# Moving the GpSimd work between the output projections and the up-projections to VectorE and ScalarE

## The chip, the cores and the metric

The kernel runs on one core of one Trainium2 chip. The metric is the device time of one execution in microseconds, as the median of several runs. Five engines run programs of their own: TensorE (PE, with its weight loads as PEld), VectorE (DVE), ScalarE (ACT), GpSimd (POOL) and SyncE (SP), which issues nearly all transfers. Each works through its own list of instructions in order, and semaphores tie the lists together.

## The reference

A trunk of two layers on 1024 positions with 1024 channels. Each layer has a mixer (even: sparse attention beside a gated convolution; odd: causal pooling beside latent attention) with one output projection, and then a convolutional FFN. Both sub-layers end in a scaled residual and a LayerNorm:

```python
h = x * (1.0 + sc_f) + sh_f
y = conv_ffn(h, ffn_w_up[l], ffn_conv_w[l], ffn_w_down[l])
x = layer_norm(DN_ALPHA * x + (1.0 + g_f) * y, ln_ffn_g[l], ln_ffn_b[l])

def conv_ffn(h, w_up, conv_w, w_down):
    u = causal_dwconv(h @ w_up, conv_w)
    val, gate = u[..., :D_FF], u[..., D_FF:]
    return (jax.nn.silu(gate) * val) @ w_down
```

D_FF is 2816, so the up-projection has 22 pairs (value and gate) of 128 columns.

## The kernel before

Positions are cut into two halves of 512 columns (`HALF`), channels into eight blocks (`KD`) of 128 partitions. A product in full precision is made of three matmuls on a high and a low half of each operand (`mm3`, L289 to L291). So every operand is first split: ACT copies the high half (`split`, L267), and DVE or POOL subtracts it from the source for the low half (L268).

The stretch that the change touches comes once in each layer:

- **Output projection** (`out_proj`). For each half, eight weight tiles `w_evo` or `w_odo` of 128x1024; the second half's low halves are POOL's. After each tile, `Norm.residual` loads the residual `xa` (in layer 0 scaled on POOL, L484), DVE adds the gated product (L495), and POOL sums the eight tiles for the mean (L505).
- **Norm**. `Norm.mean` subtracts the mean (DVE, L529), squares on ACT (L535), sums the squares on DVE and POOL in turn (L536). `Norm.var` multiplies by rstd (DVE, L556), writes the residual `xo` (ACT, L563), makes the next input `h32` (POOL, L572), and splits it to `h_f`.
- **Plain up-projections** (`Ffn.plain`). The first four pairs (`PLAIN`), half by half. The second half takes its weights' low halves from POOL. Beside it, `sums` forms the operands `t` of the Strassen products from the two halves (L772, L773, L778 and four splits on POOL). `activate` is the convolution: for each tile one ACT instruction (L701), two on DVE (L703), a silu (ACT, L707) and a product (DVE, L708).
- **Strassen up-projections** (`Ffn.strassen`). The other 18 pairs, one unit each, with seven products of 12 matmuls (84 a unit) in place of eight. `prepare` makes the operands of a unit one unit ahead: POOL forms s1 (L834, from `rawg`), s2 (L835, from s1 and `raw_upv`), s3 (L841) and s4 (L842); ACT and DVE split them. `fetch` loads `raw_upv` into one of two buffers, so that unit n's load can start when unit n-2's last reader, the split of s4 (`wl<-raw_upv`), has gone. `out` copies the products from PSUM to `u` on ACT (L873) or adds them on DVE (L871). In layer 0, `between` also works three steps of the next layer's modulation a unit, two reductions on DVE (L378) and two loads `mod_raw` to a step.

Then the down-projection (`dn`) follows, which uses `prepare` too (under the name "dn") and ends in a norm.

PE's list is written by hand. The lists of the other engines are put in order by a scheduler, by the priorities in the code (`tc.high_priority`).

Of the kernel before, what the change touches and what calls it, by code (L numbers as in the profile page):

```python
# [14 lines left out]
AF = mybir.ActivationFunctionType  # L15
# [192 lines left out]
def trunk(ctx, tc, t, out):  # L208
# [250 lines left out]
    class Norm:  # L459
# [20 lines left out]
        def residual(self, dt, ps):  # L480
            xa = self.st.tmp.tile([P, HALF], F32, tag="xa", name="xa")
            if self.first:
                load(xa, t["xT"][dt, :, half(self.hf)])
                G.tensor_scalar(xa, xa, ALPHA, 0.0, ALU.mult, ALU.add)  # L484
            else:
                load(xa, xa_dram[self.hf, dt])
            self.r[dt] = self.st.r.tile([P, HALF], F32, tag="r", name="r")
            self.gated(dt, ps, xa)
# [10 lines left out]
        def add(self, n, order=range(KD)):  # L499

            r = self.r[order[n]]
            if n:
                eng = V if self.end and n >= KD - 1 else G
                with tc.high_priority(offset=AHEAD):
                    eng.tensor_tensor(self.acc, self.r[order[0]] if n == 1 else self.acc, r, ALU.add)  # L505

# [5 lines left out]
        def mean(self):  # L512
# [14 lines left out]
            with tc.high_priority(offset=2 * AHEAD):  # L527
                for dt in range(KD):
# [4 lines left out]
                    else:  # L533
                        sq = self.tile("sq", "sq")
                        A.activation(sq, r[dt], AF.Square)  # L535
                        (G if e else V).tensor_tensor(acc[e], acc[e], sq, ALU.add)  # L536
            self.sq = acc
            defer(self.delays[1], self.var)

        def var(self):  # L540
# [14 lines left out]
            for dt in PAIRED:  # L555
# [11 lines left out]
                if self.h is None:  # L567
# [3 lines left out]
                h32 = r[dt] if self.keep else self.tile("h32", "h32")  # L571
                G.tensor_scalar(  # L572
                    h32, r[dt], f[:, 2, dt : dt + 1], f[:, 3, dt : dt + 1], ALU.mult, ALU.add
                )
# [63 lines left out]
    def out_proj(st, wsrc, k0, ysplit, gate, f, first):  # L638
        for hf in range(2):
# [4 lines left out]
            for dt in range(KD):  # L644
                src = t[wsrc][dt][:, ks[0] * P : (ks[-1] + 1) * P]
                w = weights(src, f"{wsrc}_{hf}_{dt}", lo_eng="pool" if hf else "dve")
                ps = bank("oproj")
# [22 lines left out]
    class Ffn:  # L670
# [40 lines left out]
        def plain(self):  # L711
# [3 lines left out]
            with ExitStack() as s:  # L715
# [4 lines left out]
                for hf in range(2):  # L720
# [3 lines left out]
                    for pr in range(PLAIN):  # L724
                        last = hf and pr == PLAIN - 1
                        w, ps = [], []
                        for n in range(2):
                            c = pr + n * NPAIR
                            w.append(weights(t["w_up"][l, c], f"up{l}_{hf}_{c}", "pool" if hf else "dve"))
                            ps.append(bank("up"))  # L730
# [31 lines left out]
        def sums(self):  # L762
# [5 lines left out]
            for k in range(4):  # L768
                b11, b21 = (st.tmp.tile([P, HALF], F32, tag="h32", name="blk") for _ in range(2))
                b12, b22 = st.kept[k], st.kept[k + 4]  # L770
                b = st.t[0].bitcast(F32)
                G.tensor_tensor(b11, b[:, 0, k], b[:, 1, k], ALU.add)  # L772
                G.tensor_tensor(b21, b[:, 0, k + 4], b[:, 1, k + 4], ALU.add)  # L773
                t1 = st.tmp.tile([P, HALF], F32, tag=("xa", "acc")[k // 2], name="t1")
                V.tensor_tensor(t1, b12, b11, ALU.subtract)
                V.tensor_tensor(b12, b22, b12, ALU.subtract)
                V.tensor_tensor(b22, b22, t1, ALU.subtract)
                G.tensor_tensor(b21, b21, b22, ALU.subtract)  # L778
                for dst, src in ((self.t2, b22), (self.t3, b12), (self.t4, b21)):
                    x = dst[k]  # L780
                    split(x[:, 0], x[:, 1], src, "pool" if dst is self.t4 else "dve")
                self.t1.append(t1)
# [36 lines left out]
        def prepare(self, n, name):  # L819
# [10 lines left out]

            c0, c1 = slice(0, m), slice(m, 2 * m)
            with tc.high_priority(offset=AHEAD):
                s1, s2 = (tmp.tile([P, HALF], F32, tag="s", name="s", bufs=2)[:, :m] for _ in "12")
                G.tensor_tensor(s1, g[:, c0], g[:, c1], ALU.add)  # L834
                G.tensor_tensor(s2, s1, v[:, c0], ALU.subtract)  # L835
                a = divide(v, 2 * m, f"{name}a{self.l}_{n}")
# [3 lines left out]
                split(hi[:, c1], lo[:, c1], s1)  # L840
                G.tensor_tensor(g[:, c0], v[:, c0], g[:, c0], ALU.subtract)  # L841
                G.tensor_tensor(v[:, c1], v[:, c1], s2, ALU.subtract)  # L842
                self.w = {
# [1334 lines left out]
```

## Time and profile before

| what | value |
|---|---|
| median of 3 runs | 2623.29 us (2621.45 to 2625.12) |
| the profiled execution | 2616.24 us, its span 2614.4 us |
| PE busy | 2375.9 us (91%) |
| DVE busy | 2169.9 us (83%) |
| ACT busy | 1378.1 us (53%) |
| POOL busy | 1078.8 us (41%) |

The profiled execution is 7.05 us under the median of the runs. Shares are means over the whole span; the stretch in question has values of its own. A PE that is busy isn't a PE at its peak, since matmuls overlap.

### The profile page before, as it was taken

How to read it: one execution, taken by the hardware profiler on the slowest of the kernel's cores; microseconds unless marked ns; L12 is line 12 of the kernel's file. 1: busy time of each engine (PE TensorE's matmuls, PEld its weight loads, DVE VectorE, ACT ScalarE, POOL GpSimd, SP SyncE). 2: the span in 40 equal slices, each digit the busy share in tenths (PEclk: the TensorE clock that was granted, in tenths of full speed). 3: DMA queues.
4: the chain of work that ended last, by engine and by line, in shares of the span. 5: the costliest groups of instructions: out<-in, count | busy, mean ns of one | idle time of the engine just before them, and what ended most of it. 6: DMA issues, size and time to landing. Idle time of an engine off the chain costs nothing. (4 is left out here: it accounts for less than half of the span.)

```text
span 2614.4 us, 32451 instructions
## 1 busy us (share of the span) xinstructions
PE 2375.9 (91%) x10762; PEld 1905.7 (73%) x10762; DVE 2169.9 (83%) x3495; ACT 1378.1 (53%) x2449; POOL 1078.8 (41%) x816
## 2 busy tenths in 40 slices
PE   6799997989978988998999898998989999998997
PEld 4678785877656767876787677887666888876786
DVE  7868888886898999988977868786798877788976
ACT  4558734884644344553434547675555555563434
POOL 0000003757663222324537535554675333334536
PEclk9999998999989999999999999999989999999999
DMA  6513320225434555344314331224432322244313
GB/s 249 170 42 108 97 69 17 74 77 163 133 107 159 183 172 162 104 132 151 91 55 130 93 111 39 68 80 151 138 110 93 109 84 82 93 139 140 100 48 107
DMA packets 126473, 289.44 MB, mean 111 GB/s; under 512 B 16032, under 2 KB 23712, under 8 KB 125408
## 3 DMA queue, kind: packets, MB, share of 16 engines
q1 hardware_dynamic: 125152, 283.16, 34.3%
q10 hardware_dynamic: 1152, 4.19, 0.5%
q8 instruction: 85, 1.39, 0.2%
q14 instruction: 84, 0.69, 0.1%
HBM read 234.87 MB, written 48.23 MB: 108 GB/s over the span
## 5 line engine op out<-in xcount | busy, mean ns | idle before, releaser
L703 DVE SCALAR_TENSOR_TENSOR cv<-u,taps,cv 128x512 f32<-128x512 f32 x352 | 308.4, 902 | 18.1 <-ACT cv L701 16.4
L834 POOL TENSOR_TENSOR s<-rawg 128x512 f32<-128x512 f32 (+3 forms) x60 | 78.4, 1307 | 258.8 <-DVE wlo_ups L268 87.1
L268 POOL TENSOR_TENSOR v<-v,v 128x512 fp32r<-128x512 f32 x8 | 11.9, 1492 | 416.9 <-ACT v L267 416.9
L999 DVE SCALAR_TENSOR_TENSOR r<-dn,mod,r 128x512 f32<-128x512 f32 x198 | 147.0, 745 | 41.8 <-PE dn L291 39.8
L701 ACT ACTIVATE cv<-u,taps 128x512 f32<-128x512 f32 x176 | 124.3, 721 | 56.4 <-DMA z<-cv 29.0
L289 PE MATMUL up<-t,wh 128*128 128x512 f32 x288 | 119.3, 414 | 31.5 <-ACT u L873 31.5
L707 ACT ACTIVATE cv<-cv 128x512 f32<-128x512 f32 x88 | 55.6, 632 | 144.4 <-DVE cv L703 143.5
L290 PE MATMUL up<-h_f,whi_up 128*128 128x512 f32 x256 | 105.6, 412 | 25.7 <-DVE h_f L268 25.7
L873 ACT COPY u<-up 128x512 f32<-128x512 f32 x144 | 83.9, 584 | 77.3 <-issue 33.3
L378 DVE CUSTOM_DVE_ANT_0 mod_raw<-mod_raw,cond_row 128x512 f32<-128x512 f32 (+1 forms) x112 | 106.0, 953 | 20.1 <-DMA mod_raw<-in_ada_w 16.1
L268 DVE TENSOR_TENSOR wl<-rawg,wh 128x512 fp32r<-128x512 f32 (+3 forms) x120 | 119.7, 1000 | 2.6 <-ACT wh L267 2.6
L290 PE MATMUL up<-t,wh 128*128 128x512 f32 x288 | 117.9, 409 | 0.0
L291 PE MATMUL up<-t,wl 128*128 128x512 f32 x288 | 117.6, 408 | 0.0
L835 POOL TENSOR_TENSOR s<-s,raw_upv 128x512 f32<-128x512 f32 x36 | 50.5, 1403 | 161.0 <-DMA raw_upv<-in_w_up 138.7
L267 ACT CAST wh<-rawg 128x512 fp32r<-128x512 f32 (+3 forms) x120 | 65.0, 545 | 98.2 <-PE dn L290 51.3
L289 PE MATMUL up<-h_f,whi_upa 128*128 128x512 f32 x288 | 114.5, 398 | 0.8 <-ACT whi_upa L267 0.8
L291 PE MATMUL up<-h_f,wlo_upa 128*128 128x512 f32 x288 | 113.7, 395 | 0.7 <-DVE wlo_upa L268 0.7
L290 PE MATMUL up<-h_f,whi_upa 128*128 128x512 f32 x288 | 113.0, 392 | 0.0
L268 DVE TENSOR_TENSOR pl<-pt,ph 128x128 fp32r<-128x128 f32 (+2 forms) x192 | 99.6, 545 | 14.8 <-ACT ph L267 14.1
L291 PE MATMUL up<-h_f,wlo_up 128*128 128x512 f32 x256 | 104.1, 407 | 6.0 <-POOL wlo_up L268 6.0
L842 POOL TENSOR_TENSOR raw_upv<-raw_upv,s 128x512 f32<-128x512 f32 x36 | 60.3, 1675 | 118.7 <-DVE wlo_upa L268 118.7
L289 PE MATMUL up<-h_f,whi_up 128*128 128x512 f32 x256 | 106.0, 414 | 1.6 <-ACT whi_up L267 0.8
(755 smaller groups left out, 8562.7 us busy)
## 6 DMA issues: line engine op xcount, KB each, us to landing
mod_raw<-in_ada_w SPq DMA_DIRECT2D x96, 256.0 KB, 2.9
z<-cv SPq DMA_DIRECT2D x88, 256.0 KB, 2.0
raw_upv<-in_w_up SPq DMA_DIRECT2D x36, 512.0 KB, 3.7
rawg<-in_w_up SPq DMA_DIRECT2D x34, 512.0 KB, 3.7
raw_up<-in_w_up SPq DMA_DIRECT2D x32, 512.0 KB, 3.7
z<-z SPq DMA_DIRECT2D x56, 256.0 KB, 2.7
xa_dram<-xo SPq DMA_DIRECT2D x48, 256.0 KB, 2.3
raw_dr<-in_w_dr SPq DMA_DIRECT2D x32, 384.0 KB, 3.1
```

The costliest lines, as they stand in the source:

```text
L267: A.copy(hi, src)
L268: (V if lo_eng == "dve" else G).tensor_tensor(lo, src, hi.bitcast(F32), ALU.subtract)
L289: T.matmul(ps, lhsT=wh, rhs=xh, start=start, stop=False, skip_group_check=more)
L290: T.matmul(ps, lhsT=wh, rhs=xl, start=False, stop=False, skip_group_check=more)
L291: T.matmul(ps, lhsT=wl, rhs=xh, start=False, stop=stop, skip_group_check=more)
L378: V.tensor_tensor_reduce(out=raw, in0=raw, in1=self.cond[:, o], scale=1.0, scalar=0.0, op0=ALU.mult, op1=ALU.add, accum_out=self.acc[:, j, ...
L701: A.activation(y[n], u[:, 0:HALF], AF.Copy, scale=self.taps[:, c, 0:1])
L703: V.scalar_tensor_tensor(y[n], u[:, k : k + HALF], self.taps[:, c, k : k + 1], y[n], ALU.mult, ALU.add,)
L834: G.tensor_tensor(s1, g[:, c0], g[:, c1], ALU.add)
L842: G.tensor_tensor(v[:, c1], v[:, c1], s2, ALU.subtract)
L873: A.copy(dst, ps)
L999: V.scalar_tensor_tensor(r, ps, self.gate[:, dt : dt + 1], r, ALU.mult, ALU.add)
```

## The change

All of POOL's work in this stretch goes to DVE, but for two kinds that go to ACT: the scaling of the residual in layer 0, and the next input h32. In `prepare` the four sums move for "up" alone; for "dn" they stay. `Norm` is also used at the ends of the FFNs, so its sums and h32 move there as well.

```diff
             if self.first:
                 load(xa, t["xT"][dt, :, half(self.hf)])
-                G.tensor_scalar(xa, xa, ALPHA, 0.0, ALU.mult, ALU.add)
+                A.mul(xa, xa, ALPHA)
...
             if n:
-                eng = V if self.end and n >= KD - 1 else G
                 with tc.high_priority(offset=AHEAD):
-                    eng.tensor_tensor(self.acc, self.r[order[0]] if n == 1 else self.acc, r, ALU.add)
+                    V.tensor_tensor(self.acc, self.r[order[0]] if n == 1 else self.acc, r, ALU.add)
...
-                        (G if e else V).tensor_tensor(acc[e], acc[e], sq, ALU.add)
+                        V.tensor_tensor(acc[e], acc[e], sq, ALU.add)
...
-                G.tensor_scalar(
-                    h32, r[dt], f[:, 2, dt : dt + 1], f[:, 3, dt : dt + 1], ALU.mult, ALU.add
+                A.activation(
+                    h32, r[dt], AF.Identity, bias=f[:, 3, dt : dt + 1],
+                    scale=f[:, 2, dt : dt + 1],
                 )
...
-                w = weights(src, f"{wsrc}_{hf}_{dt}", lo_eng="pool" if hf else "dve")
+                w = weights(src, f"{wsrc}_{hf}_{dt}")
...
-                            w.append(weights(t["w_up"][l, c], f"up{l}_{hf}_{c}", "pool" if hf else "dve"))
+                            w.append(weights(t["w_up"][l, c], f"up{l}_{hf}_{c}"))
...
-                G.tensor_tensor(b11, b[:, 0, k], b[:, 1, k], ALU.add)
-                G.tensor_tensor(b21, b[:, 0, k + 4], b[:, 1, k + 4], ALU.add)
+                V.tensor_tensor(b11, b[:, 0, k], b[:, 1, k], ALU.add)
+                V.tensor_tensor(b21, b[:, 0, k + 4], b[:, 1, k + 4], ALU.add)
...
-                G.tensor_tensor(b21, b21, b22, ALU.subtract)
+                V.tensor_tensor(b21, b21, b22, ALU.subtract)
...
-                    split(x[:, 0], x[:, 1], src, "pool" if dst is self.t4 else "dve")
+                    split(x[:, 0], x[:, 1], src)
...
+            eng = V if name == "up" else G
...
-                G.tensor_tensor(s1, g[:, c0], g[:, c1], ALU.add)
-                G.tensor_tensor(s2, s1, v[:, c0], ALU.subtract)
+                eng.tensor_tensor(s1, g[:, c0], g[:, c1], ALU.add)
+                eng.tensor_tensor(s2, s1, v[:, c0], ALU.subtract)
...
-                G.tensor_tensor(g[:, c0], v[:, c0], g[:, c0], ALU.subtract)
-                G.tensor_tensor(v[:, c1], v[:, c1], s2, ALU.subtract)
+                eng.tensor_tensor(g[:, c0], v[:, c0], g[:, c0], ALU.subtract)
+                eng.tensor_tensor(v[:, c1], v[:, c1], s2, ALU.subtract)
```

PE's list stays as it was. Line numbers from L485 on shift by one or two. Three places show what the scheduler made of it.

The first is DVE's list in layer 1, where unit 7 of the Strassen products is prepared and the convolution of an earlier unit (`cv`) runs; `raw_upv` is the raw value weight, `wlo_ups` the low half of s1 and s2. Before:

```order
L268 TENSOR_TENSOR wlo_ups_7_17641<-s,whi_ups_7_17640 128x512 x2
L268 TENSOR_TENSOR wl<-raw_upv_6_17391,wh 128x512
L703 SCALAR_TENSOR_TENSOR cv<-u,taps_16437,cv 128x512 x4
L914 MEMSET u 128x2
L708 TENSOR_TENSOR cv<-cv 128x512
L871 TENSOR_TENSOR u<-up,u 128x512
L268 TENSOR_TENSOR wl<-rawg,wh 128x512
```

And of the change:

```order
L268 TENSOR_TENSOR wlo_ups_7_17641<-s,whi_ups_7_17640 128x512 x2
L835 TENSOR_TENSOR s<-rawg 128x512
L268 TENSOR_TENSOR wl<-raw_upv_6_17391,wh 128x512
L703 SCALAR_TENSOR_TENSOR cv<-u,taps_16437,cv 128x512 x4
L836 TENSOR_TENSOR s<-s,raw_upv_8_17660 128x512
L842 TENSOR_TENSOR rawg<-raw_upv_8_17660,rawg 128x512
L915 MEMSET u 128x2
L708 TENSOR_TENSOR cv<-cv 128x512
L872 TENSOR_TENSOR u<-up,u 128x512
L268 TENSOR_TENSOR wl<-rawg,wh 128x512
```

The sum s2 of unit 8 (now L836) stands four convolution steps behind the split that frees the buffer for its load, and in front of the next product and the next add from PSUM.

The second is the same place in layer 0, where the reductions of the modulation (L378, here as ISA) are mixed in. Before:

```order
L268 TENSOR_TENSOR wl<-raw_upv_6_6889,wh 128x512
L703 SCALAR_TENSOR_TENSOR cv<-u,taps_5935,cv 128x512 x2
L378 ISA mod_raw,mod_acc<-mod_raw,cond_row_6922 128x512
L378 ISA mod_acc 128x1
L703 SCALAR_TENSOR_TENSOR cv<-u,taps_5935,cv 128x512 x2
L378 ISA mod_raw,mod_acc<-mod_raw,cond_row_6922 128x512
L378 ISA mod_acc 128x1
L871 TENSOR_TENSOR u<-up,u 128x512
```

And of the change:

```order
L268 TENSOR_TENSOR wl<-raw_upv_6_6889,wh 128x512
L378 ISA mod_raw,mod_acc<-mod_raw,cond_row_6922 128x512
L378 ISA mod_acc 128x1
L835 TENSOR_TENSOR s<-rawg 128x512
...
L703 SCALAR_TENSOR_TENSOR cv<-u,taps_5935,cv 128x512 x3
L872 TENSOR_TENSOR u<-up,u 128x512
L268 TENSOR_TENSOR wl<-rawg,wh 128x512
L703 SCALAR_TENSOR_TENSOR cv<-u,taps_5935,cv 128x512
L836 TENSOR_TENSOR s<-s,raw_upv_8_7200 128x512
```

Here ten instructions stand between the two (the rows left out hold one more L378 and one sum of 8 columns). From one preparation to the next the list held 9 reductions in most units before, up to unit 15; now it holds 6 or 7, up to unit 19.

The third is ACT's list in layer 0 behind the second norm's square root; `xo` is the residual, `h_f` the split input. Before:

```order
L549 ACTIVATE rstd<-ln_var,eps_ln 128x512
L267 CAST whi_up_0_3_6296<-raw_up_0_3_6294 128x1024
L743 COPY u<-up 128x512
L563 ACTIVATE xo<-r,fm_5280 128x512 x2
L701 ACTIVATE cv<-u,taps_5935 128x512
L267 CAST h_f_1_5290<-r 128x512 x2
```

And of the change:

```order
L548 ACTIVATE rstd<-ln_var,eps_ln 128x512
L562 ACTIVATE xo<-r,fm_5280 128x512 x2
L571 ACTIVATE r<-r,fm_5280 128x512
L267 CAST whi_up_0_3_6296<-raw_up_0_3_6294 128x1024
L743 COPY u<-up 128x512
L571 ACTIVATE r<-r,fm_5280 128x512
L267 CAST h_f_1_5290<-r 128x512
```

The two h32 (L571) now stand in ACT's own list, ahead of the casts that read them.

## Rows read from the trace of the kernel before

**Rows 1.** Busy time by stretch: output projection, plain, Strassen; layer 0, then 1.

```profile
584.50:658.30 73.80, 69.97 (x297) 54.99 (x296) 50.49 (x55) 32.49 (x47) 55.26 (x36) 1.00 0.52 165
658.30:779.00 120.70, 98.61 (x391) 74.93 (x390) 111.76 (x131) 66.15 (x99) 75.95 (x41) 0.93 0.33 102
779.00:1181.70 402.70, 367.40 (x1514) 292.07 (x1513) 366.98 (x605) 191.73 (x314) 129.08 (x83) 0.96 0.48 153
1792.70:1867.50 74.80, 69.92 (x298) 54.86 (x297) 49.22 (x58) 34.20 (x49) 51.53 (x31) 1.00 0.63 204
1867.50:1985.70 118.20, 98.85 (x392) 75.72 (x391) 110.14 (x128) 66.31 (x99) 72.56 (x38) 0.93 0.33 104
1985.70:2349.30 363.60, 355.82 (x1514) 286.00 (x1513) 293.17 (x391) 196.75 (x313) 130.32 (x82) 0.99 0.30 98
```

The columns are the stretch, its length, then busy time (and instructions) of PE, PEld, DVE, ACT and POOL, PE's granted clock as a share of full speed, the transfers' share and their GB/s.

**Rows 2.** The same view inside the Strassen stretches: layer 0's first units, layer 1.

```profile
795.20:1027.40 232.20, 209.73 (x856) 166.16 (x856) 215.47 (x401) 97.58 (x160) 69.74 (x44) 0.95 0.54 173
2018.00:2288.00 270.00, 270.00 (x1167) 218.76 (x1166) 214.06 (x294) 141.52 (x222) 91.40 (x59) 1.00 0.28 92
```

**Rows 3.** Who waited for whom, layer 0's Strassen stretch: total us, times, longest.

```profile
PE up L289 <- ACT u L873: 27.9, 11, 5.5
...
ACT cv L707 <- DVE cv L703: 85.2, 18, 9.3
```

**Rows 4.** Timeline of single instructions, layer 0: start, duration, engine, line.

```profile
957.93 0.69 DVE L268 TENSOR_TENSOR wl<-raw_upv,wh 128x512 fp32r<-128x512 f32 x1
...
963.83 1.76 DVE L378 CUSTOM_DVE_ANT_0 mod_raw<-mod_raw,cond_row 128x512 f32<-128x512 f32 x1
...
967.22 0.74 DVE L703 SCALAR_TENSOR_TENSOR cv<-u,taps,cv 128x512 f32<-128x512 f32 x1
967.89 0.68 DVE L378 CUSTOM_DVE_ANT_0 mod_raw<-mod_raw,cond_row 128x512 f32<-128x512 f32 x1
...
968.50 1.22 DVE L268 TENSOR_TENSOR wlo_upa<-raw_upv,whi_upa 128x1024 fp32r<-128x1024 f32 x1
...
963.25 1.79 POOL L835 TENSOR_TENSOR s<-s,raw_upv 128x512 f32<-128x512 f32 x1 [6.45 <-DMA raw_upv<-in_w_up]
```

**Rows 5.** Groups of DVE instructions, layer 0's Strassen stretch: count, busy, mean ns.

```profile
L703 DVE SCALAR_TENSOR_TENSOR cv<-u,taps,cv 128x512 f32<-128x512 f32 x141 | 110.8, 811 | 3.1 <-ACT cv L701 2.7
L378 DVE CUSTOM_DVE_ANT_0 mod_raw<-mod_raw,cond_row 128x512 f32<-128x512 f32 x96 | 86.5, 909 | 18.2 <-DMA mod_raw<-in_ada_w 14.3 <-ACT cond_row L357 3.4
L268 DVE TENSOR_TENSOR wl<-rawg,wh 128x512 fp32r<-128x512 f32 x34 | 37.4, 1103 | 0.2 <-ACT wh L267 0.2
```

**Rows 6.** The same view of the plain stretch of layer 0.

```profile
L703 DVE SCALAR_TENSOR_TENSOR cv<-u,taps,cv 128x512 f32<-128x512 f32 x29 | 33.5, 1156 | 1.9 <-ACT cv L701 1.8
L268 DVE TENSOR_TENSOR t<-r,t 128x512 fp32r<-128x512 f32 x8 | 10.6, 1358 | 0.0
L708 DVE TENSOR_TENSOR cv<-cv 128x512 f32<-128x512 f32 x7 | 10.3, 1468 | 0.7 <-ACT cv L707 0.5
```

**Rows 7.** Groups of POOL and ACT instructions in the plain stretch of layer 0.

```profile
L572 POOL TENSOR_SCALAR r<-r,fm 128x512 f32<-128x512 f32 x8 | 15.8, 1984 | 11.5 <-ACT xo L563 11.5
...
L563 ACT ACTIVATE xo<-r,fm 128x512 f32<-128x512 f32 x8 | 6.3, 806 | 1.0 <-DVE r L556 1.0
```

**Rows 8.** PE's waits in the plain stretch of layer 0.

```profile
PE up L290 <- DVE h_f L268: 12.5, 3, 10.9
PE ln_mean L515 <- POOL ln_acc L505: 3.9, 1, 3.9
```

**Rows 9.** Timeline of layer 1, DVE and POOL, where a unit's load is awaited.

```profile
2092.43 0.69 DVE L268 TENSOR_TENSOR wl<-raw_upv,wh 128x512 fp32r<-128x512 f32 x1 [1.20 <-ACT wh L267]
2093.67 2.74 DVE L703 SCALAR_TENSOR_TENSOR cv<-u,taps,cv 128x512 f32<-128x512 f32 x4 [0.55 <-ACT cv L701]
...
2097.56 0.69 DVE L871 TENSOR_TENSOR u<-up,u 128x512 f32<-128x512 f32 x1 [0.42 <-PE up L291]
...
2096.99 1.31 POOL L835 TENSOR_TENSOR s<-s,raw_upv 128x512 f32<-128x512 f32 x1 [4.62 <-DMA raw_upv<-in_w_up]
```

## The prediction

> **What bounds the kernel now.** I read the busy time by stretch first. A matmul takes its place on PE every 270.00 / 1167 = 0.231 us where PE never pauses [rows 2]. So the 1514 matmuls of a Strassen stretch need 350 us, and the 391 of a plain one 90.5. Layer 1's Strassen stretch has 363.6, so PE bounds it; layer 0's has 402.7 and the plain ones 120.7 and 118.2, where DVE is busy for 91 to 93% [rows 1]. The reader should see that the same products take 39 us more where DVE also reduces the modulation.
>
> Then the waits, for how DVE's load reaches PE. In layer 0's Strassen stretch PE waits 27.9 us for ACT's copy `u` out of PSUM. ACT is only half busy there, but its list is in order: the silu L707 waits 85.2 us for DVE's convolution [rows 3], and the copy stands behind it. In the plain stretch PE waits 12.5 us for `h_f`, a low half made on DVE, and 3.9 for POOL's sum [rows 8].
>
> Then the timeline, for why DVE is so slow. The convolution step takes 0.74 us, a reduction 0.68, a split 0.69. But a reduction that starts 0.6 us after a POOL sum takes 1.76 instead of 0.68 [rows 4]. The page's means carry the same: 811 ns for L703, 909 for L378, 1103 for the split from `rawg` [rows 5], and in the plain stretch 1156, 1358 and 1468 [rows 6]. So DVE stands still while POOL works on SBUF, and POOL's own instruction is slow too (1.79 us for 512 columns).
>
> **The change, part by part.** Neighbours on DVE overlap: L703 starts at 967.22, the next instruction at 967.89, the next at 968.50 [rows 4]. An added instruction of 512 columns therefore costs DVE 0.61 us, one of 1024 columns 1.22 less 0.08, so 1.14.
>
> *Strassen, layer 0.* Relief: 141 x 0.07 + 96 x 0.23 + 34 x 0.42 = 46 us from three rows [rows 5] against 0.74, 0.68 and 0.68; the smaller groups, stretched alike, I put at 14, so 60 in all, 3.3 a unit. Added: four sums for 18 units, 72 x 0.61 = 44 us, 2.4 a unit. The 856 matmuls of the first stretch are 10.2 units; they took 22.8 us each, 21.1 of it busy DVE [rows 2]. The new list has 6.3 reductions in such a unit instead of 9 (1.6 less, paid back in later units). That makes 21.1 - 3.3 + 2.4 - 1.6 = 18.6, against 84 x 0.231 = 19.4 of PE. DVE waited 1.6 a unit (232.2 - 215.5); part of it should stay, since both engines are now nearly full and each waits for the other now and then. I take 20.0 a unit, 0.6 over PE's: 10.2 x 2.8 = 29 gained. Six later units get the reductions and pay that 0.6 each, 4 together, and the first preparation comes 2 us sooner. Together 27. The bounds are 42 (PE's 350 and a rest of 10 for the ends) and nothing (units stay at 22.8).
>
> The sum s2 now waits on DVE for the load of `raw_upv`. In layer 1 the split ended at 2093.12 and POOL went on at 2096.99, 3.9 us later [rows 9]. In layer 0 ten instructions stand between the two, two reductions, a sum, four convolution steps, an add and a split among them: some 5.7 us by these prices, which hides it.
>
> *Strassen, layer 1.* Here only four convolution steps stand between, until 2096.41 [rows 9], so DVE waits about 0.6 us a unit, and behind it are s3, a product, and the add from PSUM that started at 2097.56. That comes 1 us late. It costs nothing as long as DVE has room: it was busy for 214.1 of 270.0, so 4.0 us a unit are free [rows 2], and the relief pays for the sums. If that room were gone, each late us would be PE's. What can be gained is in the ends of the stretch: 363.6 - 350 = 13.6, of which I take 4 for the first preparation, whose four POOL sums of 1.3 to 1.8 become 0.61 each. Bounds: 9 gained, 8 lost (18 units at 0.45).
>
> *Plain, both layers.* Relief in layer 0: 29 x 0.41 + 8 x 0.68 + 7 x 0.78 = 23 us from three rows [rows 6]; I take 31 with the smaller groups. Added to DVE: 8 low halves of weights x 1.14, 16 sums and splits for the Strassen operands, and 5 sums of the norm x 0.61: 22 us. DVE falls from 111.8 to 103 and from 110.1 to 101. The h32 leaves POOL, where it took 1984 ns, for ACT, where `xo`, the same form, takes 806 [rows 7]: 10 x 0.8 = 8 us on an engine with 66 busy of 120.7, so not on the path by its size. I take DVE's fall as the gain, 9 and 8, since DVE has the least idle time. Bounds: nothing, and 17 (the waits of rows 8 that go, and the slow clock behind them: the stretch's granted clock is 0.93).
>
> *Output projections.* PE needs 297 x 0.231 = 69 of 73.8 and 74.8 [rows 1]; eight low halves and some 16 sums go to a DVE that is busy for 50. I take 2 each, 4 together; bounds 0 and 10.
>
> *The ends of the FFNs.* Sums and h32 of the norms there move the same way. PE's wait for such a sum was 3.9 us in the plain stretch [rows 8]; three more norms like it would give 12, and nothing is the other bound. I take 4.
>
> The residual's scaling (eight, layer 0) goes to ACT, which is busy for 32 of 73.8 [rows 1]: nothing.
>
> Sum: 27 + 4 + 17 + 4 + 4 = 56 us. The profiled execution took 2616.2, so 2560; it was 7 below the median of the runs, so **2567**.
>
> **A rule against it.** By the rows, POOL's work costs DVE more (60 us) than doing it itself (44). The Trainium skill, Perfetto Trace Analysis, section Optimizing Scalar/DVE Operations, advises the reverse: if DVE is saturated, offload to ScalarE or even GpSimd. By that rule the price would be the 44 without the 60. The trace speaks against it here, since the stretch of 0.68 to 1.76 falls on POOL's sum; the same section also warns that the two share a port.
>
> **The rivals.**
>
> *PE's floor everywhere.* DVE's lists interlock better than I think: 42 + 9 + 2 x 17 + 4 + 4 = 93, so 2530. For it speaks layer 1, where DVE at 79% left PE no pause at all [rows 2]; against it that the new layer 0 has DVE at 96% of PE's time.
>
> *Little comes through.* The DVE that gets free time waits for loads and casts instead; the plain stretch ends with the same chain (norm, h32, cast, split), whose steps are now in two lists, ACT's and DVE's. Layer 0's first units take 22, and the plain stretches gain 2 each: 8 + 4 + 4 + 4 = 20, so 2603.
>
> *Slower: s2's wait.* DVE's list stands still for the load in every unit. If the load, with other transfers beside it, lands 7 us after the split and not 3.9, DVE loses 3 us more a unit. In layer 0 a unit of 18.6 + 1.6 + 3 = 23.2 is 0.4 above the old one in ten units, and 3.8 above PE's 19.4 in six: 27 lost. Layer 1 has room for it, but the add from PSUM is late by 4 us and costs perhaps 1 a unit: 18. With 21 gained elsewhere, 24 slower: 2647. It decides from about 2 us of wait a unit on. Against it: 3.9 us was measured with the same loads running.
>
> *No relief.* The stretch isn't POOL's doing, and DVE only gets the added 44, 22 and 22; the free 36 and 2 x 8 us of these stretches take up most. 88 - 52 = 36 slower, 2659. Rows 4 speak against it.
>
> **How the numbers follow.** The forecast 0.62, PE's floor 0.12, little comes through 0.14, s2's wait 0.08, no relief 0.04. Own range of the forecast: 2545 to 2592. The range that leaves out no more than 2 in 10 reaches to the first two rivals, 2534 to 2604. What a measurement tells from no change is about 0.2%, 5 us. Faster 0.85 (three cases, less a little), same 0.04, slower 0.11.
>
> **What would show it.** The convolution step back to 0.75 us in all stretches and `rawg`'s split to 0.69; layer 0's Strassen stretch at 376, its units at 20.0, ACT's wait for L703 far below 85; layer 1's at 359 with a DVE wait for `raw_upv` of about 0.6 us a unit; the plain stretches at 111 with DVE at 103 and no wait of PE for POOL. I am wrong if DVE waits for `raw_upv` for 2 us or more a unit, if PE's waits for `u` stay, or if PE's wait for `h_f` in the plain stretch stays at 11 us because the chain is now held by ACT.

## The result, and the profile after

The changed kernel took **2557.9 us** (median of 4 runs, 2556.84 to 2560.5) against 2622.37 of the kernel before beside it (4 runs): a ratio of 0.9754, 95% interval 0.9738 to 0.9771. The forecast was 2567, in a range of 2534 to 2604. The profiled execution took 2557.98 us, its span 2556.0; the profile before lay 7 us under its median, and this one lies on it.

The busy time by stretch of the changed kernel, with the columns of [rows 1]: output projection, plain and Strassen of layer 0, then of layer 1, and at the end a piece of the plain stretch of layer 0, to which I come back.

```profile
585.50:657.00 71.50, 68.84 (x296) 55.35 (x295) 59.26 (x81) 42.44 (x63) 0.00 (x0) 1.00 0.53 173
657.00:761.40 104.40, 96.38 (x391) 74.65 (x390) 92.76 (x158) 70.90 (x107) 0.00 (x0) 0.97 0.40 125
761.40:1132.40 371.00, 357.67 (x1514) 287.01 (x1513) 349.92 (x676) 190.93 (x314) 16.93 (x10) 0.98 0.51 163
1742.00:1818.40 76.40, 71.29 (x297) 55.42 (x296) 60.55 (x85) 41.29 (x59) 0.00 (x0) 0.98 0.61 202
1818.40:1922.10 103.70, 95.81 (x391) 74.59 (x390) 91.27 (x154) 69.61 (x104) 0.00 (x0) 0.97 0.39 124
1922.10:2284.40 362.30, 354.42 (x1513) 285.83 (x1512) 294.75 (x462) 195.26 (x313) 16.46 (x10) 0.99 0.30 96
...
689.80:718.00 28.20, 24.78 (x106) 19.38 (x104) 27.77 (x51) 28.17 (x45) 0.00 (x0) 1.00 0.46 141
```

Beside [rows 1], layer 0's Strassen stretch fell from 402.7 to 371.0 and the plain ones from 120.7 and 118.2 to 104.4 and 103.7; layer 1's Strassen stretch and the output projections hardly moved. In layer 0's Strassen stretch DVE does 71 instructions more and is busy for 17 us less.

The waits of the changed kernel: PE's in layer 0's plain stretch (3 rows), in layer 0's Strassen stretch (1), in the down-projection of layer 1 (2), and then DVE's in the Strassen stretch of layer 1.

```profile
PE ln_var L544 <- DVE ln_sq L535: 3.1, 1, 3.1
PE up L290 <- DVE h_f L268: 2.5, 1, 2.5
PE up L289 <- ACT h_f L267: 2.4, 1, 2.4
...
PE up L289 <- ACT u L874: 9.5, 5, 4.2
...
PE dn L289 <- DVE r L1000: 11.6, 5, 5.4
PE ln_mean L514 <- DVE ln_acc L504: 2.4, 1, 2.4
...
DVE s L836 <- DMA raw_upv<-in_w_up: 8.0, 16, 1.6
```

PE's wait for `u` went from 27.9 us [rows 3] to 9.5; ACT's 85.2 for L703 is no longer among the first seven of its waits. The 12.5 for `h_f` and the 3.9 for POOL's sum [rows 8] became three waits of 8.0 together.

Groups of DVE instructions of the changed kernel by form (count, busy, mean ns): layer 0's Strassen stretch, then its plain stretch.

```profile
L703 DVE SCALAR_TENSOR_TENSOR cv<-u,taps,cv 128x512 f32<-128x512 f32 x140 | 106.4, 778 | 2.6 <-ACT cv L701 2.4
L378 DVE CUSTOM_DVE_ANT_0 mod_raw<-mod_raw,cond_row 128x512 f32<-128x512 f32 x96 | 65.3, 683 | 1.1 <-DMA mod_raw<-in_ada_w 0.9
L268 DVE TENSOR_TENSOR wl<-rawg,wh 128x512 fp32r<-128x512 f32 x34 | 23.2, 683 | 0.2 <-ACT wh L267 0.2
...
L703 DVE SCALAR_TENSOR_TENSOR cv<-u,taps,cv 128x512 f32<-128x512 f32 x30 | 22.3, 745 | 2.7 <-ACT cv L701 2.5
L268 DVE TENSOR_TENSOR h_f<-r,h_f 128x512 fp32r<-128x512 f32 x8 | 5.4, 684 | 0.0
L268 DVE TENSOR_TENSOR t<-r,t 128x512 fp32r<-128x512 f32 x8 | 5.3, 681 | 0.0
L708 DVE TENSOR_TENSOR cv<-cv 128x512 f32<-128x512 f32 x7 | 4.8, 685 | 1.2 <-ACT cv L707 1.2
L742 DVE COPY u<-halo 128x2 f32<-128x2 f32 x16 | 2.4, 161 | 0.1
```

The means that [rows 5] and [rows 6] show as 811, 909, 1103, 1156, 1358 and 1468 are 778, 683, 683, 745, 681 and 685: nearly all of DVE's instructions have again the length that they have with POOL idle. The 778 is still a little long; in e11, with no POOL instruction left in that stretch, the same mean is 748.

### The profile page after: what moved, and what is told of

It reads as the page before. It is cut to its first block, busy times and chain, and to the rows that moved or that the text cites. A ratio compares the mean times of both kernels' runs of the same rounds, so it can differ in the third digit from the quotient of the medians.

```text
span 2556.0 us, 32216 instructions
## 1 busy us (share of the span) xinstructions
PE 2364.3 (92%) x10762; PEld 1904.7 (75%) x10762; DVE 2149.7 (84%) x3787; ACT 1409.7 (55%) x2505; POOL 527.7 (21%) x468
## 4 chain that ended last, share of the span: by engine, by line
PE 64%; DVE 19%; ACT 7%; issue 4%; DMA 4%; POOL 2%; SPq 0%; DVEq 0%; ACTq 0%; POOLq 0%
PE up L289 10%; PE up L290 10%; PE up L291 10%; PE dn L289 4%; PE dn L291 3%; PE dn L290 3%; ACT junka L1651 2%; DVE cv L703 1%; PE pt L1199 1%; DVE t L268 1%; DVE h_f L268 1%; PE oproj L289 1%; PE yps L1236 1%; PE oproj L290 1%; PE oproj L291 1%
## 5 line engine op out<-in xcount | busy, mean ns | idle before, releaser
L703 DVE SCALAR_TENSOR_TENSOR cv<-u,taps,cv 128x512 f32<-128x512 f32 x352 | 266.6, 777 | 20.9 <-ACT cv L701 19.5
L976 POOL TENSOR_TENSOR z<-z 128x512 f32<-128x512 f32 x10 | 14.9, 1488 | 935.3 <-DMA z<-z 457.2
L289 PE MATMUL up<-t,wh 128*128 128x512 f32 x288 | 114.8, 399 | 8.9 <-ACT u L874 8.9
L290 PE MATMUL up<-t,wh 128*128 128x512 f32 x288 | 114.6, 398 | 0.0
L291 PE MATMUL up<-h_f,wlo_upa 128*128 128x512 f32 x288 | 113.7, 395 | 0.0
L289 PE MATMUL up<-h_f,whi_up 128*128 128x512 f32 x256 | 103.8, 406 | 4.8 <-ACT h_f L267 4.8
L872 DVE TENSOR_TENSOR u<-up,u 128x512 f32<-128x512 f32 x108 | 74.0, 685 | 40.3 <-PE up L291 39.9
L1651 ACT ACTIVATE junka<-dd,cand 128x384 bf16<-128x384 f32 (+2 forms) x93 | 87.1, 937 | 33.3 <-DVE cand L1645 31.3
L267 ACT CAST ph<-pt 128x128 fp32r<-128x128 f32 (+2 forms) x192 | 85.2, 479 | 22.4 <-PE pt L1199 21.2
L267 ACT CAST whi_ups<-s 128x512 fp32r<-128x512 f32 x72 | 41.4, 619 | 90.3 <-PE up L290 87.2
L268 DVE TENSOR_TENSOR wl<-rawg,wh 128x512 fp32r<-128x512 f32 (+3 forms) x120 | 85.6, 715 | 2.6 <-ACT wh L267 2.6
```

The source lines that it names most:

```text
L267: A.copy(hi, src)
L268: (V if lo_eng == "dve" else G).tensor_tensor(lo, src, hi.bitcast(F32), ALU.subtract)
L289: T.matmul(ps, lhsT=wh, rhs=xh, start=start, stop=False, skip_group_check=more)
L290: T.matmul(ps, lhsT=wh, rhs=xl, start=False, stop=False, skip_group_check=more)
L291: T.matmul(ps, lhsT=wl, rhs=xh, start=False, stop=stop, skip_group_check=more)
L703: V.scalar_tensor_tensor(y[n], u[:, k : k + HALF], self.taps[:, c, k : k + 1], y[n], ALU.mult, ALU.add,)
```

## The experiments

The theory: a POOL sum that reads SBUF holds DVE up for longer than DVE needs for the sum, so what left POOL freed DVE, and through DVE PE. The rivals: the gain comes from the shorter way of the sums themselves (they no longer wait in another engine's list), or, in the plain stretch, from h32 on ACT. All runs in one table, the stretches measured from the first matmul of one to the first of the next; the down-projection up to its last matmul. A ratio is to the kernel before, run beside it; that took 2624.63 us beside e1 to e4, 2619.58 beside e5 to e8 and 2619.43 beside the last three, so runs of different sets are compared by their ratios. The stretches are those of one profiled execution each, which lay up to 8 us from the median of its kernel (e3: 2551.46 against 2559.5); with the same code, layer 0's Strassen stretch still ranged from 368.5 to 371.0, and layer 1's from 359.9 to 362.3 (the change, e4, e6, e7, e8).

| kernel | median us | ratio [95% interval] | plain 0, 1 | Strassen 0, 1 | down 0, 1 |
|---|---|---|---|---|---|
| before | 2622.4 | 1 | 120.7, 118.1 | 402.6, 363.6 | 241.9, 245.8 |
| the change | 2557.9 | 0.9754 [0.9738, 0.9771] | 104.4, 103.7 | 370.9, 362.3 | 243.2, 252.9 |
| e1, sums back | 2593.3 | 0.9876 [0.986, 0.9892] | 105.8, 104.2 | 401.8, 362.9 | 245.2, 252.1 |
| e2, idle sums | 2601.6 | 0.9913 [0.9897, 0.993] | 104.3, 103.8 | 409.4, 365.4 | 242.3, 252.1 |
| e3, idle memsets | 2559.5 | 0.9745 [0.9725, 0.9764] | 104.4, 104.5 | 369.5, 358.8 | 245.3, 253.6 |
| e4, ends back | 2555.0 | 0.9726 [0.9705, 0.9747] | 104.4, 105.4 | 368.5, 361.5 | 244.4, 247.6 |
| e5, e4 and dn's sums on DVE | 2546.7 | 0.9716 [0.9701, 0.9731] | 104.7, 104.4 | 369.9, 358.8 | 242.9, 245.6 |
| e6, h32 back | 2548.4 | 0.9723 [0.9706, 0.9739] | 97.3, 97.9 | 369.3, 361.4 | 246.0, 253.0 |
| e7, operands back | 2571.9 | 0.9814 [0.9795, 0.9833] | 113.5, 115.1 | 369.6, 359.9 | 245.9, 251.0 |
| e8, low halves back | 2566.3 | 0.9791 [0.9771, 0.981] | 113.7, 111.5 | 369.5, 359.9 | 245.7, 252.7 |
| e9, e5 and h32 back | 2539.3 | 0.9700 [0.9681, 0.972] | 97.3, 97.0 | 367.7, 360.5 | 242.6, 246.2 |
| e10, idle one-tile | 2564.8 | 0.9797 [0.9775, 0.9819] | 104.7, 103.7 | 375.9, 361.5 | 245.5, 253.1 |
| e11, e9 and all of dn on DVE | 2531.5 | 0.9671 [0.9655, 0.9688] | 97.6, 97.1 | 363.6, 357.7 | 245.5, 248.4 |

**e1: the four sums of the Strassen units back on GpSimd, all else as changed.**

```diff
-            eng = V if name == "up" else G
+            eng = G
```

> The changed kernel with the four sums of prepare back on GpSimd in the Strassen stretch alone; all else as changed. If the sums are the cause of the Strassen gain, layer 0's stretch goes from 371 back to about 400 us and the time to 2585 (2578 to 2592); layer 1's stretch stays within 3 us of 362. Rival: the gain came from a cleaner start of the stretch (plain part finished sooner, sums and h32 moved there); then this costs under 8 us, 2558 to 2566.

Layer 0's Strassen stretch is back at 401.8, with DVE at 366.62 us for 604 instructions, as before; layer 1's did not move. The time of 2593.3 is at the upper end of the theory's range. So this one part of the change carries the whole gain there, but not yet why.

**e2: the sums stay on VectorE; GpSimd gets four sums a unit that nobody waits for.** What they read and write is a tile of their own, `idle`; the copy of one column ties them to the unit.

```diff
+                if name == "up":
+                    G.tensor_copy(self.idle[:, :1], s2[:, :1])
+                    for _ in range(4):
+                        G.tensor_tensor(self.idle, self.idle, self.idle, ALU.add)
```

> The changed kernel, with four sums of 128x512 a unit added on GpSimd that nobody reads or waits for (a private tile added to itself, behind one column copied from s2). The lists of the other engines are the same, word for word. If GpSimd's work on SBUF holds VectorE up, the convolution's mean in layer 0's Strassen stretch goes back from 0.75 to over 0.80 us, that stretch to 385 to 400, the time to 2570 to 2590. Rival: what cost time before was the slow chain of sums on GpSimd that others waited for; nobody waits for these, so 2556 to 2560.

The stretch takes 409.4 us, 38 more, though no instruction of another engine depends on a sum. That is the theory's way, but beyond its 385 to 400, as the time of 2601.6 is beyond its 2570 to 2590. The busy time of the stretch, as in the result's first view, and PE's first wait in it:

```profile
760.60:1170.00 409.40, 369.63 (x1513) 293.37 (x1512) 403.32 (x676) 192.02 (x314) 137.22 (x101) 0.95 0.46 148
```

```profile
PE up L289 <- ACT u L880: 32.9, 15, 5.5
```

DVE works the same 676 instructions in 403.3 us instead of 349.9: 53.4 / 72 = 0.74 us for each idle sum. And PE's wait for `u` is back. The timeline of single instructions beside one such burst, in layer 0, POOL's row last (the form of [rows 4]; a row with x4 stands for four in a row):

```profile
894.43 0.67 DVE L378 CUSTOM_DVE_ANT_0 mod_raw<-mod_raw,cond_row 128x512 f32<-128x512 f32 x1
895.04 0.07 DVE L378 DVE_READ_ACCUMULATOR2_ANT mod_acc<- 128x1 f32 x1
895.04 0.68 DVE L878 TENSOR_TENSOR u<-up,u 128x512 f32<-128x512 f32 x1
895.64 0.91 DVE L268 TENSOR_TENSOR wl<-rawg,wh 128x512 fp32r<-128x512 f32 x1
896.48 1.53 DVE L378 CUSTOM_DVE_ANT_0 mod_raw<-mod_raw,cond_row 128x512 f32<-128x512 f32 x1
897.93 0.08 DVE L378 DVE_READ_ACCUMULATOR2_ANT mod_acc<- 128x1 f32 x1
897.93 1.52 DVE L705 SCALAR_TENSOR_TENSOR cv<-u,taps,cv 128x512 f32<-128x512 f32 x1
...
893.97 6.38 POOL L849 TENSOR_TENSOR idle<-idle 128x512 f32<-128x512 f32 x4
```

The form that takes 0.67 at 894.43 takes 1.53 at 896.48; the add L878, one of whose operands lies in PSUM (`up`), keeps its 0.68 in the middle of the burst, and its mean over the stretch is 679 ns. So the loss comes from what POOL does to DVE while it works, not from anybody's wait for a result.

**e3: the same with memsets in place of the sums.**

```diff
-                        G.tensor_tensor(self.idle, self.idle, self.idle, ALU.add)
+                        G.memset(self.idle, 0.0)
```

> The same with four memsets of 128x512 a unit in place of the four sums: they write SBUF and read nothing. If any access of GpSimd holds VectorE up, the loss goes with GpSimd's busy time, as with the sums (some 60% of that loss or more). If only instructions that read SBUF do, the time stays at 2556 to 2560.

The stretch takes 369.5 us; in 370 us of it DVE is busy for 351.4 with 677 instructions, as in the change.

```profile
760.00:1130.00 370.00, 355.95 (x1516) 285.79 (x1515) 351.40 (x677) 190.01 (x313) 68.03 (x101) 0.99 0.51 163
```

POOL writes as many tiles as in e2 and costs next to nothing. The memsets are shorter (37.9 us of POOL's time for 72, against 107.3 for the sums), but by POOL's time alone they would have cost a third of 53.4, some 19 us. So it is the reading that holds DVE up. The Trainium skill, SBUF — State Buffer, section Who interferes with whom, says just this: a DVE instruction with two SBUF inputs contends with a GpSimd instruction that reads SBUF, not with one that only writes it. On this the trace agrees, with 53 us against 1.5.

**e4: the sums of the norms at the ends of the FFNs back on GpSimd.** `ffn` is a flag that those two norms set; their h32 stays on ACT.

```diff
-                    V.tensor_tensor(self.acc, self.r[order[0]] if n == 1 else self.acc, r, ALU.add)
+                    eng = G if self.ffn and not (self.end and n >= KD - 1) else V
+                    eng.tensor_tensor(self.acc, self.r[order[0]] if n == 1 else self.acc, r, ALU.add)
...
-                        V.tensor_tensor(acc[e], acc[e], sq, ALU.add)
+                        (G if e and self.ffn else V).tensor_tensor(acc[e], acc[e], sq, ALU.add)
```

> The changed kernel with the norm's sums and sums of squares at the ends of both FFNs back on GpSimd; those of the output projections stay on VectorE, and h32 stays on ScalarE. If those sums on VectorE are what made the last stretch 6.5 us longer, it goes back to 265 us and the time to 2550 (2547 to 2553). Rival: the longer end comes from the lists' new order or h32; then 2556 to 2560.

Layer 1's down-projection falls from 252.9 to 247.6, PE's wait for `r` from 11.6 to 10.2, and the one of 2.4 for `ln_acc` inside it goes. That is more than the scatter: the seven other versions that keep these sums on DVE (e1 to e3, e6 to e8, e10) have 251.0 to 253.6 there. So in layer 1 these sums were better where they were. Layer 0's down-projection doesn't move, and from its end to the next output projection e4 takes 369.0 us where the change takes 366.5. In the whole time the step is at the edge of what the measurement tells: the intervals of e4 and of the change overlap.

**e5: e4, and the sums of the down-projections' units on VectorE too.**

```diff
-            eng = V if name == "up" else G
+            eng = V
```

> The version of e4 (sums of the FFNs' last norms back on GpSimd), with the four operand sums of each unit of the down-projections moved from GpSimd to VectorE as well; the computation is the same. Theory (a GpSimd sum costs VectorE more than the sum itself, everywhere): about 48 sums of 256 or 384 columns a layer, own cost some 0.45 us each, 22 a layer; of the 31 to 36 us by which VectorE's two-operand instructions are stretched in a down-projection, about two thirds go, 22 too. So VectorE gains little there, and the sums come sooner: the down-projections 0 to 8 us shorter each (243 and 247.6 now, 224 is PE's need), 2541 to 2555 in all. Rival (VectorE's list gets longer ahead of the evacuations that PE waits for, L1000): 3 to 6 us longer each, 2561 to 2567.

242.9 and 245.6: no more than 2 us less than e4's, the lower end of what the theory gave; the ratio falls by 0.001, less than its interval. But DVE's time, of which the theory had as much saved as added, rises: in the two down-projections it is busy for 208.5 and 214.4 us, against 200.6 and 203.6 in e4, with 50 and 53 instructions more. Here the sums cost DVE more than they save, unlike in the Strassen stretch of layer 0.

**e6: only h32 back on GpSimd.**

```diff
-                A.activation(
-                    h32, r[dt], AF.Identity, bias=f[:, 3, dt : dt + 1],
-                    scale=f[:, 2, dt : dt + 1],
-                )
+                G.tensor_scalar(
+                    h32, r[dt], f[:, 2, dt : dt + 1], f[:, 3, dt : dt + 1], ALU.mult, ALU.add
+                )
```

> The changed kernel with the next input h32 back on GpSimd, all else as changed. Question: why the plain stretches gained 16.3 and 14.5 us and not the forecast 9 and 8. Theory 1 (the chain through h32): PE's wait for h_f in a plain stretch goes from 2.5 back to about 11, the stretches are 7 to 10 us longer each (104 to 112), 2574 to 2580 in all. Theory 2 (VectorE's load alone): ten h32 a stretch hold VectorE up by about 1.07 us each, 11 us more of busy VectorE, which has 11.6 idle: 2 to 4 longer each, PE's wait for h_f under 5, 2562 to 2566.

Both theories fall: the plain stretches are 7.1 and 5.8 us *shorter* than in the change. The whole plain stretch of layer 0, and the piece of it in which the second half's `h_f` is made (689.8 to 718.0 in the change); PE's only wait; and POOL's h32:

```profile
656.60:753.90 97.30, 94.20 (x392) 73.71 (x391) 94.85 (x156) 64.32 (x96) 16.11 (x8) 0.98 0.40 131
...
688.70:709.20 20.50, 20.50 (x90) 16.48 (x89) 20.50 (x31) 16.64 (x27) 14.13 (x7) 1.00 0.44 147
```

```profile
PE ln_var L544 <- DVE ln_sq L535: 3.1, 1, 3.1
```

```profile
L571 POOL TENSOR_SCALAR r<-r,fm 128x512 f32<-128x512 f32 x8 | 16.1, 2022 | 37.0 <-ACT xo L562 37.0
```

In the change ACT is busy for 28.17 of 28.20 us in that piece: `xo`, h32, the casts of `h_f`, the copies out of PSUM and the weights' casts stand in one list, and PE waits 4.9 us for `h_f`, in this piece and right behind it. With h32 on POOL the piece takes 20.5, ACT has 3.9 free, and PE is busy throughout. The two pieces hold 106 and 90 matmuls, so the 7.1 us are better read from the whole stretch, with the same products: 4.9 are the waits for `h_f`, and PE's busy time falls by the other 2.2 (96.38 to 94.20, at a granted clock of 0.97 and 0.98). An h32 on POOL takes 2.02 us against ACT's 0.81, but POOL has nothing else to do, and DVE, with two instructions fewer in the window, is busy for only 2.1 us more: (2.1 + 2 x 0.61) / 8 = 0.41 us for each h32.

**e7 and e8: two other parts of the plain stretch back on GpSimd.** e7 the sums and splits for the Strassen operands, 16 a layer; e8 the low halves of the second half's weights, 8 in each plain stretch and 8 in each output projection.

```diff
-                V.tensor_tensor(b11, b[:, 0, k], b[:, 1, k], ALU.add)
-                V.tensor_tensor(b21, b[:, 0, k + 4], b[:, 1, k + 4], ALU.add)
+                G.tensor_tensor(b11, b[:, 0, k], b[:, 1, k], ALU.add)
+                G.tensor_tensor(b21, b[:, 0, k + 4], b[:, 1, k + 4], ALU.add)
...
-                V.tensor_tensor(b21, b21, b22, ALU.subtract)
+                G.tensor_tensor(b21, b21, b22, ALU.subtract)
...
-                    split(x[:, 0], x[:, 1], src)
+                    split(x[:, 0], x[:, 1], src, "pool" if dst is self.t4 else "dve")
```

> The changed kernel with the sums and splits that form the Strassen operands in the plain stretch (L772, L773, L778, the splits of t4) back on GpSimd: 16 instructions a layer. VectorE loses 16 x 0.61 = 10 us of its own and is held up for 16 x 1.07 = 17. Theory 1 (the plain stretch follows VectorE's load): 5 to 7 us longer each, 2568 to 2572. Theory 2 (it follows the chain through h32): within 2 us of 104.4 and 103.7, 2556 to 2562.

```diff
-                w = weights(src, f"{wsrc}_{hf}_{dt}")
+                w = weights(src, f"{wsrc}_{hf}_{dt}", lo_eng="pool" if hf else "dve")
...
-                            w.append(weights(t["w_up"][l, c], f"up{l}_{hf}_{c}"))
+                            w.append(weights(t["w_up"][l, c], f"up{l}_{hf}_{c}", "pool" if hf else "dve"))
```

> The changed kernel with the low halves of the second half's weights back on GpSimd, 8 in each plain stretch and 8 in each output projection. VectorE loses 8 x 1.14 = 9 us of its own in each and is held up for 8 x 2.1 = 17. Theory 1 (VectorE's load): plain stretches 5 to 8 us longer each, output projections 1 to 2: 2570 to 2578. Theory 2 (the chain through h32): plain stretches within 2 us, and so the output projections, 2556 to 2562.

Each makes the plain stretches longer by 8 to 11 us, somewhat more than theory 1 had. The output projections of e8 got no longer (72.1 and 73.6 us, against 71.5 and 76.4), where theory 1 had 1 to 2, and its time of 2566.3 lies between the two theories. The busy time of layer 0's plain stretch in e7, and PE's first wait in it:

```profile
656.30:769.80 113.50, 98.69 (x392) 75.58 (x391) 100.35 (x141) 71.41 (x107) 34.06 (x16) 0.92 0.37 114
```

```profile
PE up L290 <- DVE h_f L268: 10.1, 3, 5.1
```

And the same stretch in e8:

```profile
658.60:772.30 113.70, 99.40 (x392) 76.47 (x391) 100.78 (x151) 72.98 (x110) 22.13 (x8) 0.91 0.36 117
```

DVE does 17 and 7 instructions fewer than in the change (x158), and is busy for 7.6 and 8.0 us more. PE's wait for `h_f` returns, as in [rows 8], with DVE as the one that is late, and the granted clock falls from 0.97 to 0.92 and 0.91. So with h32 on ACT the plain stretch follows DVE's load, as the prediction took it. It isn't the load alone, though: in e6 DVE is busy for 2.1 us more than in the change, and the stretch is 7.1 shorter.

**e9: e5 and h32 on GpSimd.** The edits of e5 and e6 together.

> The version of e5 with the next input h32 back on GpSimd, as in e6: what the runs so far suggest as the best of the parts. Theory (the parts add up): e6 took 7.1 and 5.8 us off the two plain stretches, e5 some 9 off the layer-1 down-projection and the Strassen stretch ahead of it against the changed kernel: 2530 to 2540. Rival (both used the same slack): 2543 to 2548, as e5 and e6 alone.

2539.3, at the theory's end: the plain stretches are those of e6, the down-projections those of e5.

**e10: e2 with instructions that read one tile.**

```diff
-                        G.tensor_tensor(self.idle, self.idle, self.idle, ALU.add)
+                        G.tensor_scalar(
+                            self.idle, self.idle, self.gate[:, 0:1], self.gate[:, 1:2], ALU.mult, ALU.add
+                        )
```

> As e2 (the changed kernel with four GpSimd instructions a Strassen unit that nobody waits for), but each reads one tile instead of two: idle = idle * scalar + scalar on 128x512, the form of h32. The other engines work the same lists. Theory 1 (what holds VectorE up is the reading of tiles, and one tile costs less than half of two; e6's eight h32 in a plain stretch stretched VectorE's instructions by 3.3 us, 0.41 each): the 72 instructions cost VectorE some 30 us in layer 0's Strassen stretch instead of 77, of which a fall of 44 came through in e2: 8 to 18 us longer than 371, 2566 to 2577 in all. Theory 2 (any GpSimd instruction that reads costs the same): as e2, 405 to 412 us, near 2600. Theory 3 (a one-input instruction costs nothing, as a memset): 2555 to 2562.

```profile
763.50:1139.40 375.90, 358.96 (x1513) 287.55 (x1512) 368.84 (x676) 191.78 (x314) 165.03 (x101) 0.98 0.50 162
```

DVE's 676 instructions take 368.8 us, 18.9 more than in the change: 0.26 us for each instruction, against 0.74 in e2. The stretch is 5.0 longer, less than theory 1 had. POOL's instruction itself is longer than the sum (135.6 us for 72 of them, against 107.3), so the price doesn't go by POOL's time. With one operand tile it is about a third of that with two (the sum of e2 reads `idle` twice). The two runs differ in the operation too, so that it is the number of operands is likely and not shown. It fits h32, which has this form and does little harm on POOL (0.41 each in e6).

**e11: e9, with the rest of the down-projections' POOL work on VectorE.** The sums L976, L987, L989 and L990 and the low halves of the left-over weights.

```diff
-                G.tensor_tensor(raw[1], raw[3], raw[1], ALU.subtract)
+                V.tensor_tensor(raw[1], raw[3], raw[1], ALU.subtract)
...
-                        G.tensor_tensor(b11, t3, b11, ALU.add)
+                        V.tensor_tensor(b11, t3, b11, ALU.add)
...
-                        G.tensor_tensor(b22, b22, b11, ALU.subtract)
-                        G.tensor_tensor(b21, b21, b11, ALU.subtract)
+                        V.tensor_tensor(b22, b22, b11, ALU.subtract)
+                        V.tensor_tensor(b21, b21, b11, ALU.subtract)
...
-                    lo = "pool" if 1 else "dve"
+                    lo = "dve"
```

> The version of e9 with GpSimd's remaining work in the down-projections on VectorE too: the sums that form the operands (L976, L987, L989, L990) and the low halves of the left-over weights, some 36 instructions a layer, most of 512 columns. VectorE loses some 36 x 0.6 = 22 us of its own and is held up by 22 and 18 less. Theory: no gain and no loss of VectorE's time, the down-projections within 3 us of those of e9, 2528 to 2543. Rival (where PE waits for VectorE's evacuation L1000, more instructions in front of it cost time): 3 to 6 us longer each, 6 to 12 over e9.

The Strassen and down-projection stretches of both layers:

```profile
756.40:1120.00 363.60, 353.61 (x1513) 284.57 (x1512) 344.86 (x685) 190.10 (x313) 0.00 (x0) 1.00 0.51 167
1120.00:1365.50 245.50, 234.18 (x968) 186.28 (x968) 217.20 (x367) 91.24 (x168) 31.64 (x20) 0.97 0.33 105
1904.20:2261.90 357.70, 352.81 (x1514) 284.81 (x1513) 290.57 (x471) 195.88 (x314) 0.00 (x0) 1.00 0.30 98
2261.90:2510.30 248.40, 237.03 (x1117) 194.34 (x1115) 221.50 (x384) 93.42 (x176) 25.00 (x25) 0.97 0.31 100
```

The down-projections are 2.9 and 2.2 us longer than e9's, within the theory, but DVE is busy there for 9.1 and 7.3 us more, where the theory had no loss. The Strassen stretches are 4.1 and 2.8 shorter, 363.6 and 357.7: their last 9 POOL instructions, the first operands of the down-projection, are gone too. The four stretches together come out 1.8 us shorter. Of the 5.7 us between the two profiled spans, 4.8 lie between layer 0's down-projection and layer 1's output projection (371.1 in e9, 366.3 in e11), work that the edit hardly touches (DVE does 492 and 487 instructions there, POOL 157 and 156). So it is open how much of the gain over e9 is the edit's. This is the fastest version, 0.9671 [0.9655, 0.9688] of the kernel before; its interval just overlaps that of e9.

## Why the prediction was right

The profiled span fell by 58.4 us (2614.4 to 2556.0), where the steps of the prediction gave 56. That these meet so well is in part luck: the plain stretches gave 13.8 us more than forecast and layer 0's Strassen stretch 4.7 more, while the other steps gave 15.0 less (the 1 us that is left over lies ahead of the first of these stretches). The medians fell by 64.5 (2622.4 to 2557.9); the 7 us that the prediction added because the profile before lay under its median did not come back. By the steps:

- **POOL holds DVE up: right, and shown.** e2 makes the loss out of sums that nobody needs. The relief in layer 0's Strassen stretch, forecast as 60 us: 366.98 + 71 x 0.61 - 349.92 = 60.4 from the two rows of the stretch. Its split was less good: by the means in the result the three rows gave about 40 of the 46, so the smaller groups some 20 and not 14. The price is not the same everywhere, as e5 shows. The Trainium skill, Perfetto Trace Analysis, section Optimizing Scalar/DVE Operations, says that offloading from a saturated DVE to GpSimd may make sense. Here it doesn't: e1 is that offload, and its ratio is 0.9876 [0.986, 0.9892] against 0.9754 [0.9738, 0.9771]. The warning in the same section, that the two share an SBUF read port and that moving work between them might not help, does hold.
- **Strassen, layer 0: right.** 27 forecast, 31.7 measured, a stretch of 371.0 where 376 was written. PE still waits 9.5 us for `u`. What the nine or ten POOL instructions left in the stretch still cost is about 4 us, by e9 (367.7) and e11 (363.6).
- **Strassen, layer 1, and s2's wait: the wait right, the gain smaller.** 4 forecast, 1.3 in the profile of the change, 2.1 to 3.7 in those of e4, e6, e7 and e8, whose code for it is the same. DVE waits for `raw_upv` 8.0 us in 16 units, 0.5 a unit (0.6 was written). The timeline of the changed kernel in layer 1:

```profile
2046.39 0.69 DVE L268 TENSOR_TENSOR wl<-raw_upv,wh 128x512 fp32r<-128x512 f32 x1 [0.60 <-ACT wh L267]
2047.64 2.74 DVE L703 SCALAR_TENSOR_TENSOR cv<-u,taps,cv 128x512 f32<-128x512 f32 x4 [0.55 <-ACT cv L701]
2050.74 0.69 DVE L836 TENSOR_TENSOR s<-s,raw_upv 128x512 f32<-128x512 f32 x1 [0.36 <-DMA raw_upv<-in_w_up]
...
2052.56 0.69 DVE L872 TENSOR_TENSOR u<-up,u 128x512 f32<-128x512 f32 x1
```

  The split of `raw_upv` ends at 2047.08 and s2 starts 3.66 us later, against 3.9 in [rows 9]; 0.36 of that DVE stands idle. The add from PSUM (L872) starts 5.48 us behind the split, where it was 4.44 in [rows 9]: the 1 us late of the forecast. It cost little, since PE waited for such an add once in the stretch, for 1.2 us. The rival of s2's wait needed about 2 us a unit.
- **Plain: direction right, two terms wrong.** 9 and 8 forecast, 16.3 and 14.5 measured. First, the relief was mis-sized: I took 31 us, with 8 for the smaller groups. From the rows it was 111.76 + 7 x 1.14 + 20 x 0.61 - 92.76 = 39, since the smaller groups were stretched too. Three of them in the kernel before, same view as [rows 6]:

```profile
L268 DVE TENSOR_TENSOR h_f<-r,h_f 128x512 fp32r<-128x512 f32 x8 | 8.3, 1058 | 0.0
L777 DVE TENSOR_TENSOR r<-r,t 128x512 f32<-128x512 f32 x4 | 7.6, 1893 | 0.0
L742 DVE COPY u<-halo 128x2 f32<-128x2 f32 x16 | 6.7, 426 | 0.2
```

  At 684, 680 and 161 ns these three alone give 8 x 0.37 + 4 x 1.21 + 16 x 0.27 = 12. Second, "8 us on an engine with 66 busy of 120.7, so not on the path by its size" was wrong: ACT's work is bunched around the norm, where it has no idle time for 28 us, and h32 there costs 7.1 and 5.8 (e6). The two errors work against each other: DVE's busy time fell by 19.0 and 18.9, where 9 was forecast, and h32 on ACT took part of the gain back. With h32 left on POOL (e6) the plain stretches gain 23.4 and 20.3, both beyond the bound of 17 that I set.
- **Output projections: nothing came.** 4 forecast, 0.7 measured (2.3 shorter, 1.6 longer). The second ranged from 73.6 to 77.6 in the versions with the same code for it (e1 to e5, e7, e10), so its 1.6 says little.
- **The ends of the FFNs: wrong sign.** 4 gained forecast, 5 lost: layer 1 from its down-projection to the end is 6.4 longer, layer 0 from its down-projection to the next output projection 1.4 shorter. The step took the wait for POOL's sum as what a norm costs, and left out that the sums stand in DVE's list among the evacuations that PE waits for. In layer 1's down-projection PE's wait for `r` went from 10.5 us to 11.6, and one of 2.4 for the sum `ln_acc` came to it. e4 gives 5.3 of it back. Layer 0's down-projection, with the same edit, lost only 1.3, inside the scatter of the versions with this edit (242.3 to 246.0); why it lost no more is open.

The rival *PE's floor everywhere* (2530) was not met by the change. e11 comes near it by another way (2531.5 measured, 2537 by its ratio from the 2623.3 of the forecast): h32 and the last norms' sums back on POOL, and the down-projections' sums off it.

## What to carry to other kernels

A GpSimd instruction isn't free because its engine is idle: price it by what it adds to DVE's rows beside it, and compare that with doing it on DVE; in layer 0's Strassen stretch a GpSimd sum with two operands in SBUF cost DVE 0.74 us and the sum itself 0.61, an instruction with one only 0.26, a memset nearly nothing. The price isn't the same in every stretch: in the plain one it was about 1.1 us for each of e7's 16 instructions ((7.6 + 17 x 0.61) / 16) and 0.41 for an h32, in the down-projections less than the sums' own time (e5). So not all of an engine's work should move: the best version keeps the one-tile h32 on GpSimd. And take an engine's room from the piece of the stretch in which the work lands, since a mean of 55% busy can hide 28 us without a gap.

## What was not expected of the hardware

The price hardly goes with the time of the GpSimd instruction: 72 sums with two operand tiles added 53.4 us to DVE's busy time, 72 instructions with one 18.9, though these were longer themselves (1.88 us against 1.49), and 72 memsets 1.5. Short instructions are held up too. DVE's 16 copies of two columns in layer 0's plain stretch take 154 to 170 ns with POOL idle; in the kernel before their median was 170 and their mean 426, as a few took up to 1.23 us. One of these, with the POOL instruction beside it, in the kernel before:

```profile
725.13 1.22 DVE L742 COPY u<-halo 128x2 f32<-128x2 f32 x1
...
724.62 1.71 POOL L268 TENSOR_TENSOR t<-blk,t 128x512 fp32r<-128x512 f32 x1
```

The copy ends at 726.35, POOL's instruction at 726.33.
